# Seven products for one more K tile pair of the second MLP matrix

## The chip, the cores and the metric

The kernel runs on one core of a Trainium2 chip. The metric is the device time of one execution in microseconds (us): the median of several runs. Beside the runs there is one profiled execution, whose trace names each instruction by engine, source line and the tiles it writes and reads (`ps_d<-hi,h` writes ps_d from hi and h). Engines: TensorE (PE; its weight loads are PEld), VectorE (DVE), ScalarE (ACT), GpSimd (POOL) and SyncE (SP), whose queue issues the loads.

## The reference

A decoder trunk of two layers over 256 positions, model width 2048, hidden width 8192, all in float32. Layer 0 mixes by a gated short convolution, layer 1 by latent attention; each is followed by a squared-ReLU MLP. The change touches the two MLPs.

```python
def sq_relu_mlp(x, w1, w2):
    return jnp.square(jax.nn.relu(x @ w1)) @ w2

for layer in range(DEPTH):                       # DEPTH = 2
    mix = short_conv_mixer(...) if layer < N_A else mla_mixer(...)
    h = layer_norm(ALPHA * h + mix, ...)
    h = layer_norm(ALPHA * h + sq_relu_mlp(h, mlp_w1[layer], mlp_w2[layer]), ...)
```

## The kernel before

**Precision.** TensorE multiplies operands of type float32r, which hold fewer bits than float32. So each weight and each activation is kept as a high and a low part, `hi` and `lo` (`split`, L121 on ScalarE and L122 on VectorE), and a product is three matmuls: high times high, high times low, low times high. In `dot` (L283, L284, L285) a 128x128 piece of the activations `h` is the stationary operand and 512 columns of weights stream by. In the products of w1 (`products`, L199 and L203) the weights are stationary and 512 columns (high and low of 256 positions) or 256 columns stream.

**An MLP.** `mlp` goes through the hidden width in eight quarters of 1024 (`NQ` = 8, called quarters here for short, numbered 0 to 7). In each one, eight products of w1 give eight hidden tiles of 128 (`QC` = 8), which alternate between the PSUM banks 0 and 1 and are evacuated by `whole` (L339, L340) and `hidden` into `h`; then w2 brings them down to four blocks of 512 output columns (`NB` = 4), for two halves of 128 positions. The results of all quarters are summed in `acc`.

**Seven products.** In quarters 1 to 6 (`FAST`) the blocks 0 and 1 are done by a form of Strassen's method. A pair j of K tiles, two position halves and two blocks make a product of 2x2 by 2x2 blocks; `fast_products` does it by seven block products (`FACTORS`, named "1" to "7") in place of eight, so by 21 matmuls in place of 24. Four pairs make a quarter. Each named product has a PSUM bank of its own, over all four pairs. The left-hand combinations S1 to S4 are made once a quarter and pair by `form` (L630 to L633, then a split into `forms`); the right-hand ones are made from each pair of raw weight loads in `prepare`: a difference of 1024 columns (L154), two of 512 (L157, L160), three splits of 1024 columns and one of 512 (`t4`).

At the end of this half, `keep` (L588) adds each product to its place: "2", "3" and "4" belong to one output block each and go to `acc`; "1", "5", "7" and "6" (`OWN`) are wanted by several blocks and go to `sums` (in quarter 1 ScalarE copies them). `fold` spreads `sums` over `acc` in the last quarter, one operation per w1 product (L607).

**The direct half.** Blocks 2 and 3 are done by `down`, a block after the other: two PSUM banks (one for each half of positions), eight K tiles, six matmuls each, then `put` (L578) adds both to `acc`. Block 2 uses the banks 1 and 2, block 3 the banks 3 and 4. In the second MLP, in quarters 1 to 4, `turn_residual` transposes the residual between these two blocks on TensorE into the banks 5 and 6 (L945), and VectorE adds them (L946).

**Order.** All weights come as units of 128x1024 through one stream (`mlp_stream` sets its order): SyncE's queue loads a unit into one of five buffers `raw` (L132), ScalarE and VectorE split it into one of eight pairs `hi`, `lo`. `take` hands a unit to TensorE and prepares units up to `LOOK` = 5 ahead, a seven-product pair of units counting three. Each engine works through its own program in order and waits on semaphores; the order in each is set by the scheduler of the framework.

**Memory.** Arrays of the pool `act` lie in the order in which they are first named: c, pad0, b, a1, pad1, a2, pad2. Tag c holds `h`, b the MLP's input `xhl`, a1 `acc` (and earlier half of the input of the opening), a2 `forms`.

## Time and profile before

| | |
|---|---|
| runs | 2025.81 us median of 3 (2025.68 to 2026.14) |
| profiled execution | 2028.49 us, span 2026.4 us |
| granted clock of TensorE | 0.999 of full speed |
| HBM read | 381.25 MB, 189 GB/s over the span |

The span runs from the first to the last instruction; the execution's time holds some us around it. Rows of groups show line, engine, operation, what is written from what, shapes, count, then busy us and the mean of one in ns, then idle time ahead. Rows of the view of time show start and length in us. Rows by stretch show, for each engine, busy us and in brackets the number of instructions, then the granted clock, the DMA share and GB/s. A busy time holds the overlap of neighbours, so the pace of a stream is read from starts.

### The profile page before, as it was taken

The numbers are of one execution on the slowest core, as the hardware profiler recorded it, in microseconds if no ns is written. First come the engines' busy times: TensorE is split into PE (matmuls) and PEld (weight loads), VectorE is DVE, ScalarE is ACT, GpSimd is POOL, SyncE is SP. The second block draws the span as 40 slices with busy tenths as digits, with TensorE's granted clock in tenths as the row PEclk, the third lists the DMA queues.
The fourth block names the chain that finished last, engine by engine and source line by source line (L and its number), as shares of the span: only waits on it lengthen the run. The fifth ranks groups of instructions, "written<-read, shape, count | busy, mean of one in ns | idle before, by whom it ended". The sixth has DMA issues, their size and how long they took to land.

```text
span 2026.4 us, 30052 instructions
## 1 busy us (share of the span) xinstructions
PE 2018.3 (100%) x11240; PEld 1763.1 (87%) x11240; DVE 1605.8 (79%) x2467; ACT 1176.2 (58%) x1797; POOL 2.3 (0%) x21
## 2 busy tenths in 40 slices
PE   9999999999999999999999999999999999999998
PEld 8888888988888888888889998898888888888886
DVE  7667667787787978979678978776879798797966
ACT  6444445576565665656556655566656566565651
POOL 0000000000000000000000000000000000000000
PEclk9999999999999999999999999999999999999999
DMA  8666666564746657475654543656475664746663
GB/s 298 204 188 189 190 187 186 177 196 146 249 148 226 204 170 239 143 240 194 220 179 146 179 134 126 197 177 196 137 249 167 198 227 142 248 160 210 220 201 120
DMA packets 106849, 385.30 MB, mean 190 GB/s; under 512 B 11856, under 2 KB 12752, under 8 KB 106448
## 3 DMA queue, kind: packets, MB, share of 16 engines
q1 hardware_dynamic: 106560, 383.27, 59.3%
q8 instruction: 88, 1.44, 0.3%
q14 instruction: 57, 0.47, 0.1%
q10 hardware_dynamic: 144, 0.13, 0.0%
HBM read 381.25 MB, written 2.10 MB: 189 GB/s over the span
## 4 chain that ended last, share of the span: by engine, by line
PE 99%; DMA 0%; DVE 0%; SPq 0%; issue 0%; ACT 0%; DVEq 0%
PE ps_u L199 20%; PE ps_l L199 13%; PE ps_u L203 11%; PE ps_d L285 7%; PE ps_d L283 7%; PE ps_d L284 7%; PE ps_l L203 7%; PE ps_f L284 4%; PE ps_f L285 4%; PE ps_f L283 4%; PE ps_w L233 2%; PE ps_w L231 2%; PE ps_w L232 2%; PE ps_g L231 1%; PE ps_g L233 1%; PE ps_g L232 1%
## 5 line engine op out<-in xcount | busy, mean ns | idle before, releaser
L122 DVE TENSOR_TENSOR lo<-raw,hi 128x1024 fp32r<-128x1024 f32 x710 | 859.8, 1222 | 314.1 <-ACT hi L121 243.0
L121 ACT CAST hi<-raw 128x1024 fp32r<-128x1024 f32 x710 | 742.4, 1051 | 460.0 <-PE ps_u L199 108.0
L199 PE MATMUL ps_u<-xhl,hi 128*128 128x512 f32 x1792 | 621.0, 391 | 0.0
L203 PE MATMUL ps_u<-xhl,lo 128*128 128x256 f32 x1792 | 499.5, 280 | 0.0
L199 PEld LDWEIGHTS ps_u<-xhl,hi 128*128 128x128 f32 x1792 | 334.2, 187 | 72.4
L203 PEld LDWEIGHTS ps_u<-xhl,lo 128*128 128x128 f32 x1792 | 338.6, 189 | 1.8
L283 PE MATMUL ps_d<-hi,h 128*128 128x512 f32 x640 | 249.8, 390 | 0.0
L285 PE MATMUL ps_d<-hi,h 128*128 128x512 f32 x640 | 249.1, 389 | 0.0
L284 PE MATMUL ps_d<-lo,h 128*128 128x512 f32 x640 | 249.0, 389 | 0.0
L199 PE MATMUL ps_l<-xhl_a,hi 128*128 128x512 f32 x704 | 243.5, 392 | 0.0
L203 PE MATMUL ps_l<-xhl_a,lo 128*128 128x256 f32 x704 | 194.8, 279 | 0.0
L199 PEld LDWEIGHTS ps_l<-xhl_a,hi 128*128 128x128 f32 x704 | 131.7, 187 | 29.5
L283 PEld LDWEIGHTS ps_d<-hi,h 128*128 128x128 f32 x640 | 120.2, 188 | 25.0 <-DVE fh L340 0.3
L285 PEld LDWEIGHTS ps_d<-hi,h 128*128 128x128 f32 x640 | 120.1, 188 | 24.9
L284 PEld LDWEIGHTS ps_d<-lo,h 128*128 128x128 f32 x640 | 120.2, 188 | 24.7
L203 PEld LDWEIGHTS ps_l<-xhl_a,lo 128*128 128x128 f32 x704 | 132.2, 188 | 0.2
L199 PE MATMUL ps_l<-z,hi 128*128 128x512 f32 x240 | 83.9, 398 | 0.0
L641 ACT ACTIVATE fp<-fp 128x256 f32<-128x256 f32 x96 | 40.0, 416 | 72.6 <-DVE fp L340 71.9
L121 ACT CAST hi_t<-raw_t 128x1024 fp32r<-128x1024 f32 x48 | 50.4, 1050 | 42.9 <-DVE raw_t L154 33.4
L233 PE MATMUL ps_w<-xd,hi 128*128 128x258 f32 x256 | 73.0, 285 | 0.0
L231 PE MATMUL ps_w<-xd,hi 128*128 128x258 f32 x256 | 72.6, 284 | 0.0
L232 PE MATMUL ps_w<-xd,lo 128*128 128x258 f32 x256 | 72.4, 283 | 0.0
(257 smaller groups left out, 3134.5 us busy)
## 6 DMA issues: line engine op xcount, KB each, us to landing
raw<-in_w_dram SPq DMA_DIRECT2D x416, 512.0 KB, 4.3
raw<-in_w2f_dram SPq DMA_DIRECT2D x96, 512.0 KB, 3.6
raw<-in_w_in_dram SPq DMA_DIRECT2D x88, 512.0 KB, 3.6
raw<-in_w_out_dram SPq DMA_DIRECT2D x32, 512.0 KB, 3.9
raw<-in_w_o_dram SPq DMA_DIRECT2D x32, 512.0 KB, 4.3
raw<-in_w_kv_dram SPq DMA_DIRECT2D x10, 512.0 KB, 4.2
raw<-in_w_q_dram SPq DMA_DIRECT2D x8, 512.0 KB, 4.5
raw<-in_w_uk_dram SPq DMA_DIRECT2D x8, 512.0 KB, 4.4
```

Source lines behind the costliest of these rows:

```text
L121: nc.scalar.copy(hi, src)
L122: nc.vector.tensor_tensor(lo, src, hi.bitcast(F32), ALU.subtract)
L199: nc.tensor.matmul(ps, w[blk // 8][0][:, blk % 8, :], x, start=first, stop=False)
L203: nc.tensor.matmul(ps[:, :T], w[blk // 8][1][:, blk % 8, :], x[:, :T], start=False, stop=last)
L231: nc.tensor.matmul(ps[:, :W], hi, x[k][:, :W], start=k == 0, stop=False)
L232: nc.tensor.matmul(ps[:, :W], lo, x[k][:, :W], start=False, stop=False)
L233: nc.tensor.matmul(ps[:, :W], hi, x[k][:, W:], start=False, stop=k == NC - 1)
L283: nc.tensor.matmul(ps, x[0], w[0], start=first, stop=False)
L284: nc.tensor.matmul(ps, x[0], w[1], start=False, stop=False)
L285: nc.tensor.matmul(ps, x[1], w[0], start=False, stop=last)
L641: nc.scalar.activation(f, f, AF.Relu)
```

## The change

In quarters 1 to 6 the blocks 2 and 3 are done together, in one pass over the four K tile pairs (`MIXED` = "ppsp"): pairs 0, 1 and 3 directly ("p"), pair 2 by seven products ("s"). The four direct results have banks 1 to 4, and the products "2", "3", "4" of pair 2 go on in the banks of the results they belong to; "1", "5", "7" and "6" get the banks 0, 5, 6, 7 (`OWN_BANKS`). In a direct pair, block 3 comes first, both position halves, then block 2. `sums` holds two sets, and `fold` spreads both, in eight operations of 2x512 columns. The stream carries pair 2 as a seven-product pair of units (`w2f` now holds all blocks), the direct pairs as block 3, then block 2. In one dot of each quarter (`EVEN`: the last K tile's "22") the middle matmul is done in two of 256 columns. `turn_residual` comes after pair 0, into the banks 6 and 7. The arrays of `act` are named in the order c, a2, a1, b without pads, and a scratch area of 4096 bytes is cut to 512.

```diff
+MIXED = "ppsp"
+EVEN = (QC - 1, "22")
...
-    for tag, columns in (("c", 4096), ("pad0", 64), ("b", 8256), ("a1", 4128), ("pad1", 96), ("a2", 4128), ("pad2", 96)):
+    for tag, columns in (("c", 4096), ("a2", 4128), ("a1", 4128), ("b", 8256)):
...
+            out += [(w2f[l, q, 0, j, 0], w2f[l, q, 0, j, 1]) for j in range(QC // 2)]
+            for j, kind in enumerate(MIXED):
+                out += [(w2f[l, q, 1, j, 0], w2f[l, q, 1, j, 1])] if kind == "s" else \
+                    halves(w2[l, q, 3, j]) + halves(w2[l, q, 2, j])
...
-    def dot(ps, w, x, first, last):
+    def dot(ps, w, x, first, last, two=False):
 
         nc.tensor.matmul(ps, x[0], w[0], start=first, stop=False)
-        nc.tensor.matmul(ps, x[0], w[1], start=False, stop=False)
+        for at in (slice(0, T), slice(T, 2 * T)) if two else (slice(None),):
+            nc.tensor.matmul(ps[:, at], x[0], w[1][:, at], start=False, stop=False)
         nc.tensor.matmul(ps, x[1], w[0], start=False, stop=last)
...
     OWN, KEPT = ("1", "5", "7", "6"), (2, 3, 4, 5, 6, 7, 0)
+    OWN_BANKS = (0, 5, 6, 7)
...
-        sums = fast.tile([P, 4, BW], F32, name=f"sums{idx}")
+        sums = fast.tile([P, 4, 2, BW], F32, name=f"sums{idx}")
...
+            ps = {p: psum("ps_d", bank) for p, bank in zip(("22", "3", "2", "4"), (1, *KEPT))}
+            for j, kind in enumerate(MIXED):
+                if kind == "s":
+                    first, last = j == MIXED.index("s"), j == MIXED.rindex("s")
+                    if first:
+                        ps.update({p: psum(f"ps_f{p}", bank) for p, bank in zip(OWN, OWN_BANKS)})
+                    fast_products(ps, h, forms, j, OWN if first else (), OWN if last else ())
+                    if last:
+                        for p in OWN:
+                            keep(p, 1, ps[p])
+                    continue
+                for nb, two in ((3, ((1, "22"), (0, "3"))), (2, ((0, "2"), (1, "4")))):
+                    w, = take(1)
+                    for t, p in two:
+                        for kk in range(2):
+                            k = 2 * j + kk
+                            dot(ps[p], wide_rows(w, kk), held(h[k], t), k == 0, k == QC - 1, (k, p) == EVEN)
+                    if j == n - 1:
+                        for _, p in two:
+                            keep(p, 1, ps[p])
+                if extra and q <= NB and j == 0:
+                    for t in range(2):
+                        extra(block, q - 1, t, KEPT[4 + t])
...
-                first_pair(h, forms, KEPT)
-                for n, banks in ((2, (1, 2)), (3, (3, 4))):
-                    down(h, put, n, banks)
-                    if extra and n == 2 and q <= NB:
-                        for t in range(2):
-                            extra(block, q - 1, t, 5 + t)
+                down_pairs(h, forms)
...
-    nc = _bacc.Bacc("TRN2", target_bir_lowering=False, num_devices=1, dynamic_dma_scratch_size=4096)
+    nc = _bacc.Bacc("TRN2", target_bir_lowering=False, num_devices=1, dynamic_dma_scratch_size=512)
```

More of the change, by code (lines that the diff above doesn't have):

```diff
@@ L83, in mlp_stream @@
             out += halves(w1[l, q * QC:(q + 1) * QC])
-            plain = halves(w2[l, q, 2:] if q in FAST else w2[l, q])
-            fast = [(w2f[l, q, j, 0], w2f[l, q, j, 1]) for j in range(QC // 2)] if q in FAST else []
-            at = 0 if q or q not in FAST else len(plain) // 2
-            out += plain[:at] + fast + plain[at:]
+            if q not in FAST:
+                out += halves(w2[l, q])
+                continue
[3 more added lines that the diff above has]
+                    halves(w2[l, q, 3, j]) + halves(w2[l, q, 2, j])
         return out
@@ L333, in fast_products @@
         for p, l, r in FACTORS:
-            dot(ps[p], b[r], a[l], j == 0, j == n - 1)
+            dot(ps[p], b[r], a[l], p in fresh, p in ready)
     def whole(ps, out):
@@ L588, in keep, with down_pairs @@
                 nc.vector.tensor_tensor(at, at, ps, ALU.add)
-        def first_pair(h, forms, banks):
+        def down_pairs(h, forms):
             n = QC // 2
-            ps = {p: psum(f"ps_f{p}", bank) for (p, _, _), bank in zip(FACTORS, banks)}
+            ps = {p: psum(f"ps_f{p}", bank) for (p, _, _), bank in zip(FACTORS, KEPT)}
             for j in range(n):
-                fast_products(ps, h, forms, j, n)
+                fast_products(ps, h, forms, j, ps if j == 0 else (), ps if j == n - 1 else ())
@@ L599, in fold @@
         def fold():
             s1, s5, s7, s6 = (sums[:, i] for i in range(4))
[L602 to L606 removed]
+            c = acc.rearrange("p t (g b c) -> p t b g c", g=2, b=2)
```

23 lines of the change are left out of this document (12 added, 11 removed).

## The prediction

> **What bounds the kernel now.** I read the page first: the busy times, then the chain that ended last by engine.
>
> ```profile
> span 2026.4 us, 30052 instructions
> PE 2018.3 (100%) x11240; PEld 1763.1 (87%) x11240; DVE 1605.8 (79%) x2467; ACT 1176.2 (58%) x1797; POOL 2.3 (0%) x21
> PE 99%; DMA 0%; DVE 0%; SPq 0%; issue 0%; ACT 0%; DVEq 0%
> ```
>
> TensorE is busy for the whole span and is the chain. Next I asked for the waits of TensorE alone:
>
> ```profile
> PE ps_g L199 <- ACT hi L121: 1.9, 1, 1.9
> PE offset L998 <- DVE udiag L996: 1.2, 1, 1.2
> PE warm L355 <- DVE col L357: 1.1, 1, 1.1
> ```
>
> Three waits, 4.2 us in all, none in the quarters that the change touches. So the time is the number of matmuls times their pace, for as long as VectorE and ScalarE deliver in time. The busy times by stage say how near that is. The rows are, for two quarters of the first MLP in turn, the eight products of w1 and then the two halves of w2 (seven products on blocks 0 and 1, direct on blocks 2 and 3):
>
> ```profile
> core 0: us, PE busy (x) PEld busy (x) DVE busy (x) ACT busy (x) POOL busy (x), PEclk, DMA share, GB/s
> 587.70:606.80 19.10, 19.10 (x87) 15.79 (x86) 17.69 (x24) 11.19 (x15) 0.00 (x0) 1.00 0.53 159
> 606.80:628.50 21.70, 21.70 (x97) 18.00 (x96) 19.11 (x21) 12.63 (x12) 0.00 (x0) 1.00 0.82 290
> 628.50:672.90 44.40, 44.40 (x257) 39.09 (x257) 35.27 (x52) 27.57 (x45) 0.00 (x0) 1.00 0.55 171
> 672.90:692.00 19.10, 19.10 (x86) 15.81 (x85) 17.55 (x25) 12.26 (x16) 0.00 (x0) 1.00 0.54 162
> 692.00:713.80 21.80, 21.80 (x98) 18.05 (x97) 18.92 (x21) 11.59 (x11) 0.00 (x0) 1.00 0.84 314
> ```
>
> VectorE has some 2.8 us free in the direct half and 9.1 us in the 44.4 us of products. The clock is 1.00 throughout.
>
> **What is removed.** The view of time gives TensorE's pace: its rows at the start and the end of a half follow each other without a gap.
>
> ```profile
> 682.72 0.39 PE L284 MATMUL ps_f<-lo,forms 128*128 128x512 f32 x1
> 691.79 0.39 PE L285 MATMUL ps_f<-t,h 128*128 128x512 f32 x1
> 692.01 0.39 PE L283 MATMUL ps_d<-hi,h 128*128 128x512 f32 x1
> ```
>
> From 682.72 to 692.01 are 41 steps: 9.29/41 = 0.2266 us each (the 0.39 is one matmul's own length; they overlap). The third K tile pair of blocks 2 and 3 took 8 dots of 3 matmuls and now takes 7, so 3 go. That happens in six quarters of two layers: 36 x 0.2266 = 8.16 us. In one dot of each quarter a 512 column matmul becomes two of 256. Two such in a row stand in the trace where the w1 products turn their order:
>
> ```profile
> 543.88 0.40 PE L203 MATMUL ps_u<-xhl,lo 128*128 128x256 f32 x2
> 544.12 0.64 PE L199 MATMUL ps_u<-xhl,hi 128*128 128x512 f32 x2
> 544.59 0.28 PE L203 MATMUL ps_u<-xhl,lo 128*128 128x256 f32 x1
> ```
>
> The two take 0.24 us, 0.013 over one of 512, and the two of 512 behind them 0.47, 0.017 over. Cost 0.02 to 0.04 us; I take 0.035, 0.4 us for twelve. The sum for TensorE alone is 7.75 us.
>
> The Trainium skill ("TensorE: Matmul & The Clock Gate", Back-to-back issue gap) gives about 131 ns a matmul at 512 columns for a sustained stream of weight loads and matmuls. By it the saving would be 36 x 0.131 = 4.7 us; this trace's 0.2266 differs and decides.
>
> **What is added, and what hides it.** The third pair's weights now go through the seven-product preparation. Its VectorE operations, from the groups of one half by shape:
>
> ```profile
> L122 DVE TENSOR_TENSOR lo_t<-raw_t,hi_t 128x1024 fp32r<-128x1024 f32 x2 | 2.4, 1222 | 0.0
> L160 DVE TENSOR_TENSOR raw<-raw 128x512 f32<-128x512 f32 x2 | 1.4, 688 | 0.0
> L157 DVE TENSOR_TENSOR raw<-raw,raw_t 128x512 f32<-128x512 f32 x2 | 1.4, 686 | 0.0
> L122 DVE TENSOR_TENSOR t<-raw,t 128x512 fp32r<-128x512 f32 x2 | 1.4, 683 | 0.0
> L154 DVE TENSOR_TENSOR raw_t<-raw,raw 128x1024 f32<-128x1024 f32 x1 | 1.2, 1220 | 0.0
> ```
>
> Added per quarter: L154 1.22, one more split 1.22, three operations of 512 columns at 0.69: 4.5 us. Eight sums instead of four leave PSUM in the direct half, 4 x 0.68 = 2.7 us more (0.68: rows of L588 below). ScalarE gets one more cast of 1024 columns and one of 512. The loads stay two of 512 KB in the same place of SP's queue, from another array. In the direct half VectorE then needs 18.9 + 7.2 = 26.1 us, while TensorE takes 21.1. So 5.0 us are carried into the products, which have 9.1 free: hidden, if no single result comes too late. That is to be followed along VectorE's order, which I read from the changed program. Up to the sum of product 1 it is the order of before, so the trace shows it, at 692.01 as start of the half:
>
> ```profile
> 691.93 1.23 DVE L122 TENSOR_TENSOR lo<-raw,hi 128x1024 fp32r<-128x1024 f32 x1 [1.33 <-ACT hi L121]
> 693.07 0.68 DVE L588 TENSOR_TENSOR sums<-sums,ps_f 128x512 f32<-128x512 f32 x1
> 693.66 1.22 DVE L122 TENSOR_TENSOR lo<-raw,hi 128x1024 fp32r<-128x1024 f32 x1
> 694.80 1.28 DVE L588 TENSOR_TENSOR sums<-sums,ps_f 128x512 f32<-128x512 f32 x2
> 696.00 0.68 DVE L588 TENSOR_TENSOR acc<-acc,ps_f 128x512 f32<-128x512 f32 x1
> 696.59 0.68 DVE L588 TENSOR_TENSOR sums<-sums,ps_f 128x512 f32<-128x512 f32 x1
> 697.19 0.68 DVE L588 TENSOR_TENSOR acc<-acc,ps_f 128x512 f32<-128x512 f32 x1
> ```
>
> A new wait stands here. Banks 3 and 4 held products 1 and 5 and were wanted again only after 48 matmuls; now the direct sums "2" and "4" open them after 12 and 18 matmuls: 12 x 0.2266 = 2.72 us and 4.08 us. Product 1's sum ends at 693.75, 1.74 us into the half: 1.0 us to spare. Product 5 follows at once and ends by 2.4. The sum stands behind a split that waits for ScalarE's cast, which waits for a DMA or for TensorE; all TensorE work would queue behind that. The worst quarter of the trace is the one at 606.78:
>
> ```profile
> 606.78 0.39 PE L283 MATMUL ps_d<-hi,h 128*128 128x512 f32 x1
> 608.21 1.23 DVE L122 TENSOR_TENSOR lo<-raw,hi 128x1024 fp32r<-128x1024 f32 x1 [2.52 <-ACT hi L121]
> 609.35 0.68 DVE L588 TENSOR_TENSOR sums<-sums,ps_f 128x512 f32<-128x512 f32 x1
> ```
>
> There it ends 3.25 us in, 0.5 late. The wait's cost is between 0 and 0.5 us a quarter; one quarter in twelve looks like that one, so I take 0.3 us in all and keep 6 us as its upper bound.
>
> Next is the third pair itself. Step to step VectorE needs 1.14 us for 1024 columns (693.66 to 694.80) and 0.60 for 512 (696.00 to 696.59). After product 1 the six other sums end the queue at 1.65 + 6 x 0.6 = 5.3 us; the chain of the third pair (first split, difference, two of 512, two splits, last of 512) reads 6.4, 7.6, 8.2, 8.8, 9.9, 11.1, 11.7. TensorE begins the pair at 48 x 0.2266 = 10.9 us and wants those splits at 11.1, 12.5, 13.8 and 15.2: 2.6 us or more to spare, 1.1 in the worst quarter. Then follow ten splits of the next products and eight sums up to the first evacuation of a w1 product: 11.7 + 2 x 1.14 + 10 x 1.14 + 8 x 0.6 = 30.2. Bank 0 is wanted again two products later, at 21.1 + 11.1 = 32.2 (a product is 44.4/8 = 5.55): 2 us to spare, 0.5 in the worst. By the eighth product the 5 us are worked off. So I put these at nothing; without that cover the cost is the 5.0 us carried over, per quarter.
>
> In the second MLP the turned residual goes to banks 6 and 7 after 24 matmuls rather than 48. Products 2 and 6 have left those by 3.5 and 4.1 us by the same spacing, against 5.4. The final fold gets eight operations of 1024 columns for four of 512 and two of 1024: 9.8 - 5.2 = 4.6 us in 44 us of products with 9 free, twice.
>
> **The other arrays.** Without pads, one array alone (a1: the first half of the opening's input, the accumulator, half of an attention input) changes its place relative to the others within 512 bytes. The trace shows the same loop at two paces with inputs in the same place (below), so place is not what it shows to matter; bounds 0 and, for the opening's 48 column blocks with eight K tiles each from a1, 384 pairs x 0.0076 = 2.9 us. I take 0.
>
> **Sum.** 8.16 - 0.4 - 0.3 = 7.5 us. The profiled execution took 2028.49 us, 2.1 around its span of 2026.4, and would take 2021.0; it stands 2.7 above the median of 2025.81, so the median becomes 2018.3.
>
> **The rivals.** First, the bank wait bites in most quarters: 12 x 0.5 = 6 us eaten, 2024.0. For it: VectorE's order there is fixed and its split waits for others. Against: a typical quarter has 1.0 us to spare.
>
> Second, the products of w1 fall into the slower pace. Pairs of one 512 and one 256 matmul:
>
> ```profile
> 299.79 0.40 PE L199 MATMUL ps_l<-z,hi 128*128 128x512 f32 x1
> 302.27 0.40 PE L199 MATMUL ps_l<-z,hi 128*128 128x512 f32 x1
> 559.62 0.39 PE L199 MATMUL ps_u<-xhl,hi 128*128 128x512 f32 x1
> 561.70 0.39 PE L199 MATMUL ps_u<-xhl,hi 128*128 128x512 f32 x1
> ```
>
> Seven pairs in 2.48 us against six in 2.08: 0.3543 and 0.3467. If the new end of the half tips the twelve stages behind it, 12 x 128 x 0.0076 = 11.7 us are lost: 2025.8 - 7.5 + 11.7 = 2030.0. Against: the split stands 18 matmuls of 512 ahead of the stage, and each quarter's matmuls change by an even number.
>
> Third, slower: VectorE's lead is gone before the third pair, so the 5.0 us are not carried but waited for. It decides once the chain above starts 2.6 us later than worked out. Price 12 x 5.0 = 60 us less 7.5: 2078. For it: VectorE would be busy for 93% of a quarter (35.27 + 17.55 + 18.92 + 7.2 of 85.3 less 0.7). Against: the margins above.
>
> Fourth, a bank wait in each quarter is followed by a stretch at a lower granted clock, as one row of the opening has it:
>
> ```profile
> 10.00:15.00 5.00, 4.80 (x18) 4.22 (x19) 4.80 (x13) 4.79 (x15) 0.00 (x0) 0.68 1.05 431
> ```
>
> Five us at 0.68 lose 1.6; twelve lose 19: 2025.8 - 7.5 + 19 = 2037. Against: a wait of half a us would have to do it, and all stages quoted above stand at 1.00. The Trainium skill ("TensorE: Matmul & The Clock Gate", A second HAM failure mode: psum-queue depth-cycling) tells of such a kernel, whose short idles between groups in changing banks let the clock swing; nothing here shows it yet.
>
> That the change does not do what it says (a1's place costs the whole bound) gives 2021.2, within the first range.
>
> **How the numbers follow.** Forecast 2017.0 to 2021.5: 0.76. Bank waits, 2021.5 to 2026: 0.10. Slower pace: 0.06. VectorE late: 0.05. Clock: 0.03. The range 2017.0 to 2023.0 holds the first and half of the second. A change of 0.2% (4.05 us), about what this kernel's runs can tell, needs less than 2021.8 or more than 2029.9. Faster 0.77 (the forecast and a little of the second), same 0.12 (the rest of the bank waits, half of the slower pace), slower 0.11 (the other half, VectorE, clock).
>
> **What would show it.** Right: 11216 matmuls, the direct half 0.65 us shorter, no TensorE wait over 0.5 us at the direct sums, VectorE near 1695 us (1605.8 + 12 x 7.2 + 2 x 4.6, less what ScalarE copies). Wrong: TensorE waiting at the direct sums of bank 3, at the third pair's splits, or at a w1 product's bank; or 0.354 us a pair in the w1 stages.

## The result and the profile after

The changed kernel takes 2029.78 us, the median of 20 runs, against 2026.14 us for the kernel before in the same session: a ratio of 1.0019 (95% interval 1.0012 to 1.0025), 3.6 us slower where 7.5 us less were forecast. Its runs also lie further apart: 2026.82 to 2033.91 us, while those of before lie between 2025.66 and 2026.60, apart from a single one of 5211.27.

The page of the profiled execution after, the busy times and the chain by engine:

```profile
PE 2014.6 (99%) x11216; PEld 1756.3 (87%) x11216; DVE 1682.4 (83%) x2571; ACT 1191.9 (59%) x1829; POOL 2.3 (0%) x21
PE 84%; DVE 9%; DMA 3%; issue 2%; ACT 1%; SPq 0%; DVEq 0%; ACTq 0%
```

The 24 matmuls are gone from the count (36 less, 12 more by the two-part matmul), and VectorE's busy time is near the 1695 us forecast. But the chain has left TensorE: 9% of it is now VectorE and 3% DMA, where before had 0% of each. TensorE's waits, in us, times, and the longest:

```profile
PE ps_u L204 <- DVE fp L347: 2.3, 3, 1.1
PE ps_d L288 <- DVE sums L596: 2.1, 4, 0.9
...
PEld ps_d L288 <- ACT hi L126: 4.6, 6, 1.3
PEld ps_u L204 <- DVE fp L347: 3.8, 5, 1.5
```

Both kinds of place are named: a direct sum that opens a bank (ps_d), and a w1 product that opens one (ps_u); the weight load of such a matmul (PEld) shows the same stall, put down to the cast that came last. The stretches that answer to those of before, and one of the second MLP as the last:

```profile
583.60:602.68 19.08, 19.08 (x87) 15.77 (x85) 18.06 (x24) 11.40 (x17) 0.00 (x0) 1.00 0.54 163
602.68:624.12 21.44, 21.39 (x95) 17.44 (x94) 19.55 (x23) 11.41 (x12) 0.00 (x0) 1.00 0.65 223
624.12:668.52 44.40, 44.40 (x258) 39.15 (x257) 39.31 (x57) 28.55 (x47) 0.00 (x0) 1.00 0.60 199
668.52:687.60 19.08, 19.08 (x87) 15.78 (x85) 18.89 (x26) 12.31 (x17) 0.00 (x0) 1.00 0.52 153
687.60:709.86 22.26, 21.37 (x95) 17.44 (x94) 19.89 (x25) 11.62 (x12) 0.00 (x0) 1.00 0.67 230
1754.10:1799.91 45.81, 44.66 (x258) 39.15 (x256) 41.23 (x60) 29.68 (x47) 0.00 (x0) 1.00 0.60 197
```

The direct half should take 21.11 us (93 steps of 0.2266 and the split); here it takes 21.44 and 22.26. The w1 stage of the last row takes 45.81 instead of 44.39. Added up over the trace from the first matmul of each stage to the first of the next:

| | before | after |
|---|---|---|
| up to the first w1 stage with two banks | 458.07 | 454.62 |
| twelve direct halves, turned residual included | 264.7 | 261.4 (256.9 without a wait) |
| fourteen w1 stages, over 44.39 each | 0.0 | 6.8 |

So the halves save 7.8 us and give 4.5 back in waits, and the w1 stages give back 6.8: 11.3 us lost against 7.8 saved. The 3.45 us at the start are no gain of the mechanism: 2.7 of them lie in the opening's first groups, which took 26.3 us in the profile of before, 23.6 in that of after, and between 23.3 and 26.4 in the profiles of the experiments, whatever their arrays, and before's profiled execution was some 2.4 us over its own median. That of after (2027.96 us) was 1.8 under its median, so in a common run the waits are probably larger than in this trace.

### The profile page after: what moved, and what is told of

It is laid out like the page before. It is cut to its first block, busy times and chain, and to the rows that moved or that the text cites. A ratio compares the mean times of both kernels' runs of the same rounds, so it can differ in the third digit from the quotient of the medians.

```text
span 2026.2 us, 30145 instructions
## 1 busy us (share of the span) xinstructions
PE 2014.6 (99%) x11216; PEld 1756.3 (87%) x11216; DVE 1682.4 (83%) x2571; ACT 1191.9 (59%) x1829; POOL 2.3 (0%) x21
## 4 chain that ended last, share of the span: by engine, by line
PE 84%; DVE 9%; DMA 3%; issue 2%; ACT 1%; SPq 0%; DVEq 0%; ACTq 0%
PE ps_u L204 16%; PE ps_l L204 13%; PE ps_u L208 8%; PE ps_l L208 7%; PE ps_d L288 6%; PE ps_d L291 5%; PE ps_d L290 5%; DVE lo L127 3%; DMA raw<-in_w_dram 3%; PE ps_f L291 3%; PE ps_f L290 3%; PE ps_f L288 3%; PE ps_w L238 2%; PE ps_w L236 2%; PE ps_w L237 2%
## 5 line engine op out<-in xcount | busy, mean ns | idle before, releaser
L288 PE MATMUL ps_d<-hi,h 128*128 128x512 f32 x556 | 218.2, 392 | 2.3 <-DVE sums L596 2.1
L291 PE MATMUL ps_d<-hi,h 128*128 128x512 f32 x556 | 216.8, 390 | 0.0
L290 PE MATMUL ps_d<-lo,h 128*128 128x512 f32 (+1 forms) x568 | 216.7, 385 | 0.0
L288 PEld LDWEIGHTS ps_d<-hi,h 128*128 128x128 f32 x556 | 104.5, 188 | 26.4 <-ACT hi L126 4.6
L290 PEld LDWEIGHTS ps_d<-lo,h 128*128 128x128 f32 x568 | 106.7, 188 | 21.7
L291 PEld LDWEIGHTS ps_d<-hi,h 128*128 128x128 f32 x556 | 104.4, 188 | 21.5
L126 ACT CAST hi_t<-raw_t 128x1024 fp32r<-128x1024 f32 x60 | 62.8, 1047 | 97.6 <-DVE raw_t L159 96.7
L159 DVE TENSOR_TENSOR raw_t<-raw,raw 128x1024 f32<-128x1024 f32 x60 | 73.2, 1220 | 7.6 <-DMA raw<-in_w2f_dram 7.4
L127 DVE TENSOR_TENSOR lo_t<-raw_t,hi_t 128x1024 fp32r<-128x1024 f32 x60 | 73.2, 1220 | 1.2
L238 PE MATMUL ps_w<-xd,hi 128*128 128x258 f32 x256 | 72.8, 285 | 0.0
```

What stands on the lines that cost most here:

```text
L126: nc.scalar.copy(hi, src)
L127: nc.vector.tensor_tensor(lo, src, hi.bitcast(F32), ALU.subtract)
L159: nc.vector.tensor_tensor(t.rearrange(two, a=2), b12.unsqueeze(1).to_broadcast([P, 2, BW]), r1.rearrange(two, a=2), ALU.subtract)
L238: nc.tensor.matmul(ps[:, :W], hi, x[k][:, W:], start=False, stop=k == NC - 1)
L288: nc.tensor.matmul(ps, x[0], w[0], start=first, stop=False)
L290: nc.tensor.matmul(ps[:, at], x[0], w[1][:, at], start=False, stop=False)
```

## The experiments

Times are medians; every call had runs of the kernel before on the same chip, which came out between 2026.14 and 2026.50 us. "Lost" is what a profile shows over the lengths without a wait: in the twelve direct halves, and in the w1 stages. It holds for the profiled execution, which lies within 2 us of the median but for three runs: that of "both" took 2031.24 us, 5.5 over its median, that of "layout4" 3.9 over, that of "pool2" 4.4 over. "onet4" lost another 1.3 us in the twelve seven-product halves, "pool" and "pool2" 15.5 each.

| run | us | range | ratio to before (95%) | lost: halves, w1 |
|---|---|---|---|---|
| after | 2029.78 | 2026.8 to 2033.9 | 1.0019 (1.0012 to 1.0025) | 4.5, 6.8 |
| banks | 2029.69 | 2026.9 to 2031.7 | 1.0016 (1.0007 to 1.0024) | 9.3, 3.7 |
| order | 2029.70 | 2027.8 to 2033.7 | 1.0016 (1.0007 to 1.0025) | 0.0, 13.4 |
| both | 2025.78 | 2020.5 to 2033.0 | 0.9998 (0.9990 to 1.0007) | 1.9, 12.0 |
| layout | 2026.47 | 2025.5 to 2028.8 | 1.0001 (0.9993 to 1.0010) | 0.2, 0.0 |
| dose12 | 2028.46 | 2027.7 to 2029.8 | 1.0012 (1.0003 to 1.0021) | 3.7, 0.0 |
| prep | 2033.16 | 2031.7 to 2033.8 | 1.0033 (1.0020 to 1.0046) | 4.8, 2.7 |
| nosums | 2024.03 | 2022.2 to 2028.5 | 0.9989 (0.9980 to 0.9997) | 1.4, 3.9 |
| raw6 | 2018.77 | 2018.3 to 2020.6 | 0.9963 (0.9951 to 0.9976) | 1.4, 0.0 |
| raw6order | 2018.13 | 2017.7 to 2018.9 | 0.9960 (0.9945 to 0.9975) | 1.4, 0.0 |
| onet4 | 2032.95 | 2031.9 to 2035.2 | 1.0034 (1.0022 to 1.0045) | 12.1, 1.9 |
| early | 2038.51 | 2036.9 to 2043.3 | 1.0064 (1.0051 to 1.0077) | 23.6, 0.4 |
| place | 2025.07 | 2024.7 to 2027.2 | 0.9995 (0.9986 to 1.0004) | 0.0, 0.0 |
| place6 | 2028.29 | 2027.0 to 2032.3 | 1.0012 (1.0003 to 1.0022) | 2.2, 0.0 |
| layout4 | 2031.38 | 2030.4 to 2035.2 | 1.0029 (1.0019 to 1.0040) | 5.1, 0.0 |
| even | 2030.92 | 2027.4 to 2034.2 | 1.0023 (1.0014 to 1.0032) | 6.4, 9.5 |
| stall | 2032.48 | 2031.3 to 2033.6 | 1.0032 (1.0022 to 1.0043) | 0.0, 5.1 |
| pool | 2103.22 | 2102.4 to 2103.9 | 1.0380 (1.0366 to 1.0394) | 47.8, 22.5 |
| pool2 | 2102.37 | 2101.6 to 2106.7 | 1.0375 (1.0361 to 1.0390) | 49.0, 24.7 |

### Give the two places more room: banks, order, both

If the fault were the two late hand-overs of banks, other banks and another order would cure it. "banks":

```diff
-                for m, ps in enumerate(products(QC, xhl, TURNED, (0, 1))):
+                for m, ps in enumerate(products(QC, xhl, TURNED, (0, 5, 6, 7, 0, 5, 0, 1))):
```

> After, but the eight products of each w1 stage take banks 0, 5, 6, 7, 0, 5, 0, 1 in turn instead of 0 and 1; nothing else. Theory (VectorE enters each seven-product half some 1.7 us later than before and so evacuates late; a TensorE wait at a w1 product's bank also tips that stage into the slower pace): no wait at a w1 product's bank, every w1 stage at 44.4 us, which takes away the 6.8 us that six such stages of the profile had over it; the waits at bank 3 of the direct half stay (4 to 5 us). 2029.8 - 6.8 = 2023.0, at most 2024.5. Rival (VectorE is simply too late; the wait moves on to the next thing it delivers): the w1 stages stay long, 2028 to 2030.

"order" (the stream is reordered to match, and the turned residual follows block 3):

```diff
                 for nb, two in ((3, ((1, "22"), (0, "3"))), (2, ((0, "2"), (1, "4")))):
-                    w, = take(1)
...
+                    for i in (0, 1) if j == 0 else (j,):
+                        w, = take(1)
...
```

> After, but the first two K tile pairs of blocks 2 and 3 are taken block by block (block 3 of both pairs, then block 2 of both), so that banks 3 and 4 open 24 and 36 matmuls into the half (5.44 and 8.2 us) instead of 12 and 18. Theory: no wait at bank 3 any more, the first part of the direct half is 10.9 us in each quarter (4.5 us less in all); but TensorE then comes earlier to the w1 products, whose banks 0 and 1 are still handed on late, so part or all of it comes back there with the slower pace behind it: 2026 to 2030. Rival (the two waits are independent of each other): 2029.8 - 4.5 = 2025.3 or less, w1 stages as long as in the profile of after.

> Both of these edits together. Theory (the lost time is these two bank waits and the pace behind them): all direct halves 21.1 us, all w1 stages 44.4, 2029.8 - 4.5 - 6.8 = 2018.5, at most 2020. Rival (VectorE has too much work for its place, and the wait moves to the third pair's splits or to the splits of w1): waits there of 0.3 us or more in half of the quarters, 2022 to 2027.

Neither alone gained anything. TensorE's waits in "banks", then in "order":

```profile
PE ps_d L288 <- DVE sums L596: 7.1, 7, 1.6
PE ps_u L204 <- DVE fp L347: 2.2, 4, 1.3
```

```profile
PE ps_u L206 <- DVE fp L349: 4.3, 3, 2.2
```

With more banks in w1 the waits grew at the direct sums, from 4.5 to 9.3 us of the halves. With the direct sums out of the way (their halves all at 21.11 in the first MLP) they came back twice as large in w1, 13.4 us, some 1.6 of it by a stretch at a lower clock (last section). The profiles lose 13.0 us in "banks" and 13.4 in "order", that of after 11.3: the wait moves to wherever VectorE's result is wanted next. Both edits together did gain: 4.0 us less than after in the median, with intervals that don't overlap, and runs from 2020.5 to 2033.0; the 13.9 us of the profile belong to one of the slowest of them. So the two margins are part of the loss, but with both widened most of it stayed: my theory, which had 2018.5, fell in its size, and the rival holds, that VectorE is late as such.

### Where VectorE is late: layout, dose12, prep, nosums

"layout" keeps the one pass, the eight banks and their early opening, and leaves out the third pair's seven products:

```diff
-MIXED = "ppsp"
+MIXED = "pppp"
-EVEN = (QC - 1, "22")
+EVEN = (QC, "22")
```

> After with the third pair of blocks 2 and 3 computed directly like the others (8 dots instead of 7, no preparation, no second set of four sums, no two-part matmul); the one pass over both blocks with banks 1, 2, 3, 4, the order of the arrays and the products' banks stay as in after. Theory (VectorE's 4.5 + 2.7 us a quarter make it late): bank 3 is ready as in the traced halves of before, 1.0 us ahead; no wait over 0.3 us there in most quarters, w1 stages at 44.4: the time of before or up to 2 us less, 2024 to 2026.5. Rival (opening banks 3 and 4 so early is a wait by itself, whatever VectorE has to do): waits of 0.3 us or more at bank 3 in most quarters, 2028 or more.

No wait came (0.2 us in all halves), and the time is that of before: opening banks 3 and 4 early costs nothing while VectorE has before's work. "dose12" then puts the change's time on VectorE back, and nothing else of it:

```diff
+                if j == 1:
+                    for i in range(12):
+                        nc.vector.tensor_tensor(sums[:, i % 4, 1, :], block(0, 0), block(0, 0), ALU.add)
```

> The kernel of the run 'layout' (all of the third pair direct, no waits, 2026.5) with twelve operations of 512 columns put into VectorE's order at the place of the second pair, 12 x 0.6 = 7.2 us a quarter, into a buffer that nobody reads. Theory (VectorE's added time alone makes the loss): the evacuations lag by 5 us and more and TensorE waits at bank 3 and at w1 banks from the second or third quarter of each MLP on; 4 to 11 us slower than 'layout', 2030 to 2037. Rival (the third pair's loads and casts, or its earlier wants of banks 0, 5, 6, 7, make the loss): 2028 or less.

It lost 2.0 us by the medians (3.5 by the two profiles), less than the theory's least of 4 and close to the rival's most: VectorE's busy time (1684.6 us) is that of after, and most of the loss is missing. "prep" has the same time on VectorE by the change's own preparation: the third pair is loaded and prepared as for seven products, with four such operations beside it, and TensorE's stages stay as in "layout":

```diff
-                out += [(w2f[l, q, 1, j, 0], w2f[l, q, 1, j, 1])] if kind == "s" else \
+                out += [(w2f[l, q, 1, j, 0], w2f[l, q, 1, j, 1])] if j == 2 else \
...
+                    b, = take(1)
+                    for i in range(4):
+                        nc.vector.tensor_tensor(sums[:, i % 4, 1, :], block(0, 0), block(0, 0), ALU.add)
```

> The run 'layout' (5 raw buffers) with the third pair of blocks 2 and 3 loaded and prepared as for seven products, three raw buffers held as in after, plus four operations of 512 columns for the four sums: VectorE's and ScalarE's work and the buffers are those of after, while TensorE still does 8 dots with no further banks. The third pair's dots take prepared differences in place of plain weights, so that part of the result is not the reference's. Theory R (the held buffers, beside VectorE's time, make the lag): clearly more lost than the 2.0 us of 'dose12', which had the same time on VectorE and no buffer held: 2030.5 or more. Rival V (VectorE's time alone; after loses more only because its stages are 0.65 us shorter and its banks wanted earlier): as 'dose12', 2027.5 to 2029.5.

6.7 us over "layout", with VectorE busy for 1677.1 us, less than in "dose12". So VectorE's busy time alone doesn't set the loss; the preparation costs by what else it brings: raw buffers held, casts that wait for VectorE, and another order on both engines. One row of ScalarE's waits differs between the two, first in "dose12" and then in "prep":

```profile
ACT hi_t L126 <- DVE raw_t L159: 33.3, 12, 2.8
```

```profile
ACT hi_t L126 <- DVE raw_t L159: 96.0, 24, 6.0
```

The cast of a pair's difference stands in ScalarE's order until VectorE has written the difference; with a third pair it stands there twice as often and up to 6.0 us long, and the casts of plain weights queue behind it. After has the same row with 96.7, 24 and 6.0, before 33.4, 12 and 2.8. Three raw buffers are held meanwhile. The standing by itself isn't the loss: "raw6" below keeps twelve such waits of up to 6.6 us, 66.5 in all, and loses only 1.4 us.

VectorE's time still counts where the rest is given. "nosums" leaves out the sums of the third pair after the first such quarter:

```diff
-                    if last:
+                    if last and q == 1:
```

> After, but the four product sums of the third pair are added only in the first such quarter of each MLP and left out in the others: VectorE has 4 x 0.6 = 2.4 us less in ten quarters. This leaves a part of the result out. Theory V: the lag per quarter shrinks by up to 2.4 us and most of the waits go: 2020 to 2024. Theory R: the loads are as late as before, 2027 to 2030.

5.7 us less than after, for 2.4 us in each of ten quarters.

### The raw buffers: early, raw6, onet4, place6, layout4

```diff
-        t4 = r1[:, :BW]
+        t4 = t[:, :BW]
```

> After, but a pair's last difference (t4) is written into the first half of the buffer t instead of the first half of the first load's buffer r1, which so comes free some 3 us sooner for the next load; no work is added or removed. Theory R (VectorE's idle time is the five raw buffers: the third pair holds three of them to the end of its preparation, the loads behind start late, and VectorE stands in order behind a cast that waits for them): VectorE's waits for casts shrink, evacuations lag less, 2022 to 2026. Rival V (VectorE's added work, and stages 0.65 us shorter, alone set its lag): 2029 to 2030.5, as after.

It went the other way, to 2038.51 us. One buffer comes free sooner, but the last difference now stands behind the cast and the split of t, and the other two come free later; the run neither speaks for theory R nor against it.

```diff
-RAW, WA = 5, 8
+RAW, WA = 6, 8
...
-        f = state["fast"].tile([P, 2, BW], F32R, tag="t4", name=f"t4_{i}", bufs=2)
+        f = state["fast"].tile([P, 2, BW], F32R, tag="t4", name=f"t4_{i}", bufs=1)
```

> After with six raw buffers instead of five, paid for with one t4 buffer instead of two. Theory R: one more load under way, the casts wait less for loads, lag at the first evacuation back to 3 to 4 us: 2019 to 2024. Rival V: no change beyond what the missing t4 buffer costs, 2029 or more.

2018.77 us: with as many instructions on each engine, 11 us less than after and 7.7 less than before, within 0.5 us of the time that I had forecast for the change. The page, the only wait in the MLPs that the view of TensorE's waits names, and one quarter of the second MLP (w1, seven products, direct half):

```profile
PE 2008.8 (100%) x11216; PEld 1755.1 (87%) x11216; DVE 1676.3 (83%) x2571; ACT 1198.3 (59%) x1829; POOL 2.3 (0%) x21
PE 96%; DVE 2%; DMA 1%; issue 0%; ACT 0%; SPq 0%; DVEq 0%
```

```profile
PE ps_d L288 <- DVE acc L596: 0.4, 1, 0.4
```

```profile
1748.50:1792.89 44.39, 44.39 (x258) 39.12 (x256) 36.91 (x55) 27.18 (x43) 0.00 (x0) 1.00 0.53 178
1792.90:1811.98 19.08, 19.08 (x87) 15.77 (x86) 18.42 (x26) 13.60 (x19) 0.00 (x0) 1.00 0.59 188
1811.98:1833.50 21.52, 21.41 (x96) 17.43 (x95) 21.45 (x27) 10.63 (x11) 0.00 (x0) 1.00 0.68 242
```

VectorE has as much to do as in after and is no longer late: in the direct half it is busy for 21.45 of 21.52 us, in after for 19.55 of 21.44 and 19.89 of 22.26. What changed is how long ScalarE's casts stand waiting for a load, in after and then in "raw6":

```profile
ACT hi L126 <- DMA raw<-in_w_dram: 126.4, 131, 3.6
```

```profile
ACT hi L126 <- DMA raw<-in_w_dram: 62.9, 92, 2.5
```

Half of that waiting is gone. Before had 87.6 us of it. (The row by itself is no measure of the loss: in "dose12" it has 165.3 us, where the twelve operations in a row hold up the buffers.) The edit has two parts, so each was tried by itself or elsewhere. "onet4" has the single t4 buffer without the sixth raw buffer:

> After with one t4 buffer instead of two, and five raw buffers as in after: the half of the run 'raw6' that pays for the sixth. Theory R (the sixth raw buffer alone makes the 11 us of 'raw6'): the time of after or more, 2029 to 2034. Rival (one t4 buffer changes VectorE's order for the better): 2019 to 2024.

"place6" gives both to "place", the kernel before with the new order of the arrays (below), which has no waits to lose:

> The run 'place' (before with the arrays in the new order) with six raw buffers and one t4 buffer, as in 'raw6'. TensorE has no wait there to lose. Theory: 2025.1 within 0.7, so that with six buffers the change itself is worth 2025 less 2018.8 = 6.3 us, about what 36 matmuls and the waits left over make. Rival (a sixth buffer speeds up the kernel as such, by another way than the waits of the change): 2022 or less.

The single t4 buffer costs 3.2 us in after and the pair of edits costs 3.2 in the kernel "place". So the sixth raw buffer is worth 14.2 us (2032.95 less 2018.77) where the third pair is prepared, while the same two edits make the kernel without it no quicker. One reserve: VectorE's order follows from the buffers and is another one in each of these versions. In "raw6" the sums of products 3 and 1 follow each other without a split between:

```profile
1811.72 1.23 DVE L127 TENSOR_TENSOR lo<-raw,hi 128x1024 fp32r<-128x1024 f32 x1 [0.53 <-ACT hi L126]
1812.87 0.68 DVE L596 TENSOR_TENSOR acc<-acc,ps_f 128x512 f32<-128x512 f32 x1
1813.46 1.87 DVE L596 TENSOR_TENSOR sums<-sums,ps_f 128x512 f32<-128x512 f32 x3
```

How much of the gain comes with that order wasn't separated from the earlier loads.

"layout4" (`RAW, WA = 4, 8` in "layout") takes a buffer away where VectorE has nothing more to do:

> The run 'layout' (the third pair direct, no added work on VectorE, no waits) with four raw buffers instead of five. Theory R (what a quarter can carry is set by the loads through the raw buffers, not by VectorE's time): the waits of after come back without any added work, at the direct sums and at w1 banks, VectorE's busy time unchanged: 2032 or more. Rival V (VectorE's time sets it): 2026 to 2028, as 'layout'.

4.9 us are lost by the medians at an unchanged busy time (1608.2 us), but not where the theory said. The profile, the slowest of the eight runs, shows none in the first MLP, 5.1 us in the second around the turned residual, and about as much in the attention, which also loads through these buffers. That fewer buffers cost time is shown; that they alone make after's picture isn't.

"raw6order" joins "raw6" and "order":

> The run 'raw6' with blocks 2 and 3 taken block by block over the first two pairs, as in the run 'order'. With the loads in time, the rest of the waits at the direct sums (1.4 us in the profile of 'raw6') has 2.7 us more room: 2017.4 to 2018.5. Rival (TensorE, no longer held there, meets the late evacuation in w1 instead): 2018.8 or more.

2018.13 us (17.7 to 18.9) is the least of all, though the 1.4 us in the halves that it was to take away are still there: at best 0.6 us better than "raw6", and their ranges overlap. I had them at the wrong place: in "raw6" TensorE waits six matmuls into the half, where "3" opens bank 2 behind the evacuation of product 3, and "order" opens that bank no later.

### The pace, the arrays, GpSimd: stall, even, place, pool

In after, five of the fourteen w1 stages run at 0.354 us a pair from their third product on, 0.65 to 0.7 us each. "stall" makes a wait at the same place in the kernel before:

```diff
-                for m, ps in enumerate(products(QC, xhl, TURNED, (0, 1))):
+                for m, ps in enumerate(products(QC, xhl, TURNED, (0, 0, 1, 0, 1, 0, 1, 0))):
```

> Before, but the second product of each w1 stage goes into the bank of the first (0, 0, 1, 0, 1, 0, 1, 0), so that TensorE has to wait there once in each of fourteen stages, some 2.5 us. Theory (a TensorE wait inside a w1 stage tips the pairs behind it into the slower pace): the six products behind the wait at 0.354 us a pair instead of 0.347 in most stages, 0.7 us a stage beside the wait. Rival (the slower pace in after is chance or comes from something else): 0.347 behind the waits too.

The view of time of "stall" around such a place, in the w1 stage that starts at 541.77:

```profile
546.99 0.39 PE L199 MATMUL ps_u<-xhl,hi 128*128 128x512 f32 x1
...
549.76 0.39 PE L199 MATMUL ps_u<-xhl,hi 128*128 128x512 f32 x1
549.99 0.28 PE L203 MATMUL ps_u<-xhl,lo 128*128 128x256 f32 x1
550.12 0.19 PEld L199 LDWEIGHTS ps_u<-xhl,hi 128*128 128x128 f32 x1 [0.16 <-DVE fp L340]
550.12 0.50 PE L199 MATMUL ps_u<-xhl,hi 128*128 128x512 f32 x1
550.46 0.28 PE L203 MATMUL ps_u<-xhl,lo 128*128 128x256 f32 x1
550.57 0.40 PE L199 MATMUL ps_u<-xhl,hi 128*128 128x512 f32 x1
...
553.40 0.40 PE L199 MATMUL ps_u<-xhl,hi 128*128 128x512 f32 x1
```

Eight pairs ahead take (549.76 - 546.99)/8 = 0.346 us, eight behind (553.40 - 550.57)/8 = 0.354. The first product ends at 547.34, but its bank is opened again only at 550.12: by the count of matmuls, eight pairs of another product have been put between. So the wait that I expected at 2.5 us was next to none: the matmul at 550.12 starts 0.13 us after the last one, and the step behind it is 0.34 long instead of 0.23. Thirteen stages tipped at this place and one at the next such hand-over, 48 matmuls on, each where a bank just let go was opened; the thirteen fell back to 0.347 two or three products later, by what wasn't found. That TensorE opens a bank so soon after its product, and not the late release, does it isn't excluded here; in after the product had ended 5.55 us before.

"even" leaves out the two-part matmul (`EVEN = (QC, "22")`):

> After without the two-part matmul: the half has an odd number of matmuls. Theory (TensorE's pace in a w1 stage goes by how the stage is entered): w1 stages without a wait take 44.4 us in one quarter and 45.2 in the next; since VectorE's lag eats what TensorE gains, the time is that of after within 3 us. Rival (the split does nothing for the pace): all stages without a wait at 44.4, 0.4 us less than after.

The w1 stages at 455.2 and 539.7, and those at 1412.3 and 1497.8, all stand at 44.39 with an odd number of matmuls between them: no parity shows. The halves without a wait take 21.08 instead of 21.11, so the split costs 0.03 us, as I had put it, and buys nothing that shows here.

"place" has only the arrays' order and the small scratch:

> Before with only the new order of the arrays (no pads) and the smaller scratch. Theory (the 384 pairs with z run at the quicker pace for it, as in the profile of after, and nothing else moves): 1 to 3 us less than before. Rival (the place of the arrays means nothing, the pace there is chance): the time of before, within 0.5 us.

The stage of the products with z, in "place" and in before:

```profile
280.09:363.30 83.21, 83.21 (x482) 73.36 (x481) 63.21 (x103) 44.68 (x61) 0.00 (x0) 1.00 0.64 187
```

```profile
281.57:366.35 84.78, 84.78 (x482) 73.58 (x481) 63.92 (x103) 44.61 (x61) 0.00 (x0) 1.00 0.62 185
```

1.57 us less in that stage, 0.65 more in the products of the opening ahead of it (245.17 for 244.52): 0.9 us less in all, and so it is in each of the eighteen profiles with the new order against the two with the old, before and "stall". The time is 1.25 us less, though the interval of the ratio reaches 1.0004.

"pool" moves the four small operations of `form` to GpSimd, and "pool2" issues their split still later:

```diff
-                nc.vector.tensor_tensor(s1, a21, a22, ALU.add)
+                nc.gpsimd.tensor_tensor(s1, a21, a22, ALU.add)
...
```

> After, but the four 128x128 operations that build the sums of a pair's factors (sf) run on GpSimd instead of VectorE, and their two-part split is issued one product later; VectorE has 16 x 0.2 to 0.28 = 3.2 to 4.5 us less to do in each quarter. Theory (VectorE has no usable time for the 7.2 us that the change adds; its lag, not the banks, is the cause, so the waits only moved in the two runs with other banks and another order): with half of the dose gone the first evacuation of a w1 product lags its end by 3.5 us or less instead of 5 to 6.6, no wait over 0.3 us at bank 3 or at a w1 bank: 2018 to 2020. Rival (the lag is that of loads through the five raw buffers and of casts behind them, so less work on VectorE buys nothing, or GpSimd is so slow that VectorE waits for it): 2026 or more.

> The run with the factor sums on GpSimd again, with their two-part split issued a further product later (that of the last pair inside the seven-product half), since there GpSimd's four operations took 3.6 us in a row and VectorE and ScalarE waited for them in each pair. VectorE has 3.2 to 4.5 us less per quarter. Theory V: half of the dose gone, 2020 to 2025. Theory R: VectorE's work does not matter, 2028 to 2030. Third: GpSimd's chain still stops the queues: over 2035.

Both took 2102 to 2107 us. GpSimd's groups in "pool", and VectorE's split of the hidden tile between 700 and 1000 us, in after and in "pool":

```profile
L660 POOL TENSOR_TENSOR sf<-fp 128x128 f32<-128x128 f32 x48 | 52.3, 1089 | 242.1 <-ACT fp L677 242.1
```

```profile
L127 DVE TENSOR_TENSOR h<-fp,h 128x512 fp32r<-128x512 f32 x12 | 8.2, 685 | 0.0
```

```profile
L127 DVE TENSOR_TENSOR h<-fp,h 128x512 fp32r<-128x512 f32 x12 | 11.4, 950 | 0.0
```

An operation that VectorE does in 0.29 us took GpSimd 1.09, and VectorE's split beside it grew from 0.69 to 0.95 us. The Trainium skill ("SBUF — State Buffer", Who interferes with whom) says that a VectorE instruction with two inputs in SBUF and a GpSimd instruction that reads SBUF hold each other up; the row agrees. ScalarE's cast of the sums waited for GpSimd 2.0 us in each of the 48 pairs (97.4 us), with all casts of weights behind it. The runs say nothing on VectorE's time.

## Why the prediction was wrong

**TensorE's saving: right.** 11216 matmuls, and a direct half without a wait takes 21.11 us for 21.76, 12 x 0.65 = 7.8 us. With six raw buffers the kernel reaches 2018.77; the forecast was 2018.3. That these lie so close is in part luck: the order of the arrays gives 0.9 us that I had put at nothing, and 1.4 us of waits are left. The granted clock stayed at 1.00 in the stages of after; the fourth rival didn't come there. By the rule of the Trainium skill ("TensorE: Matmul & The Clock Gate", Back-to-back issue gap), about 131 ns a matmul, the estimate for the 36 was 4.7 us; the halves without a wait show 7.8.

**VectorE's added work: right in size, wrong in when it can be done.** 1682.4 us against 1695. The step that failed is this: "In the direct half VectorE then needs 18.9 + 7.2 = 26.1 us, while TensorE takes 21.1. So 5.0 us are carried into the products, which have 9.1 free: hidden, if no single result comes too late", and with it the chain worked out behind it, where each step of VectorE follows the last without a gap. It lets VectorE fill the 2.8 us that it stood idle in the direct half. In after it didn't: it is busy for 19.2 us of a direct half on average and idle for 2.6, in before for 19.2 and 2.8. VectorE's waits in the half that starts at 692.01 in before, and in the one that starts at 687.60 in after:

```profile
DVE lo L122 <- ACT hi L121: 4.2, 4, 1.5
```

```profile
DVE lo L127 <- ACT hi L126: 2.3, 4, 1.5
```

VectorE stands in its order behind a split whose cast hasn't come, and in both the casts wait mostly for loads (5.8 and 6.1 us in these two halves). Over the twelve halves these waits of VectorE's come to 34.8 us in before, 34.7 in after and 4.4 in "raw6", where VectorE is idle for 0.4 us a half. So nearly the whole 7.2 us of added work, and not 5.0, was pushed behind the half. The 9.1 us in the products were for the most part what I took them for. VectorE's waits in that stage of before (628.5 to 672.9), and in that of after (624.1 to 668.5):

```profile
DVE lo L122 <- ACT hi L121: 8.7, 7, 1.5
```

```profile
DVE lo L127 <- ACT hi L126: 4.0, 4, 1.4
```

In before the casts there waited for TensorE (7.7 us), so VectorE was ahead of it, and after did use about half of that time: it is busy for 39.31 us there instead of 35.27, 4.9 more on average over quarters 2 to 6. But the results came too late for the banks, and in after the casts wait for loads there too (3.7 us, where before has none). The loads are the term that I had put at nothing, with no more said than that they "stay two of 512 KB in the same place of SP's queue": the third pair holds three of five raw buffers while it is prepared, and leaves two to the loads behind it. Beside that it has casts that wait for VectorE themselves; since "raw6" keeps the longest of these and loses only 1.4 us, the buffers weigh more. Nor were the 5 us "worked off" by the eighth product. That VectorE entered the next seven products late, the evacuation of the last w1 product shows, before and then after, 2.3 us into the half that starts at 672.93 and 4.1 into the one that starts at 668.52:

```profile
675.24 0.42 DVE L340 TENSOR_TENSOR fp<-ps_u,t 128x256 f32<-128x256 f32 x1
```

```profile
672.59 0.42 DVE L347 TENSOR_TENSOR fp<-ps_u,t 128x256 f32<-128x256 f32 x1
```

The experiments divide the loss roughly. After's time without any wait would be some 2017.3 us ("place" less the 7.75 of TensorE's sum), so 12.5 are lost. By the medians VectorE's time alone makes 2.0 of them ("dose12"), the preparation around it 4.7 more ("prep"); the other 5.8, by that subtraction alone (4.4 if it starts from "layout", whose median is 1.4 over that of "place"), I put down to stages 0.65 us shorter and banks wanted sooner. No run shows that part by itself.

**Product 1's sum: the mechanism seen, the place right, the size wrong.** I gave it 1.0 us to spare in a typical quarter and 0.3 us of loss in all. In after, in the quarter whose half starts at 687.60:

```profile
688.32 1.05 ACT L126 CAST hi<-raw 128x1024 fp32r<-128x1024 f32 x1 [2.29 <-DMA raw<-in_w_dram]
...
689.40 1.23 DVE L127 TENSOR_TENSOR lo<-raw,hi 128x1024 fp32r<-128x1024 f32 x1 [1.52 <-ACT hi L126]
...
690.54 1.88 DVE L596 TENSOR_TENSOR sums<-sums,ps_f 128x512 f32<-128x512 f32 x3
...
691.37 0.47 PE L288 MATMUL ps_d<-hi,h 128*128 128x512 f32 x1 [0.89 <-DVE sums L596]
```

Read from top to bottom: a load comes late, the cast waits 2.29 us for it, the split 1.52 us for the cast, the three sums stand behind the split, and TensorE waits for the first of them, which ends 3.6 us into the half and was wanted at 2.72. VectorE isn't short of time here; it stands idle for 1.52 us just ahead. In the traced quarter of before the same split started 0.08 us ahead of the half, here 1.80 behind its start. That is the third rival's condition, VectorE's lead gone, but not its price: no half of after shows a wait at the third pair's splits. I had taken the lateness of the worst quarter of before as an outlier of one in twelve; in after eight of twelve halves wait there, 4.5 us in all.

**The first evacuation of a w1 product: the second margin, whose cost I put at nothing.** I had it end 30.2 us after the start of the direct half, with bank 0 wanted at 32.2. In the stage that starts at 1754.10 (the half before it at 1731.80):

```profile
1760.37 5.76 DVE L127 TENSOR_TENSOR lo<-raw,hi 128x1024 fp32r<-128x1024 f32 x5
...
1763.75 1.05 ACT L126 CAST hi<-raw 128x1024 fp32r<-128x1024 f32 x1 [1.47 <-DMA raw<-in_w_dram]
...
1766.05 0.42 DVE L347 TENSOR_TENSOR fp<-ps_u,t 128x256 f32<-128x256 f32 x1
...
1766.52 0.50 PE L204 MATMUL ps_u<-xhl,hi 128*128 128x512 f32 x1 [1.15 <-DVE fp L347]
```

It ends at 1766.47, 34.7 us after the start of the half, 4.5 later than worked out; TensorE, whose half is 1.2 us longer than 21.11 (0.9 of it the turned residual), wanted the bank at 1765.2. VectorE works without a gap from 1756.84 on, at the end through five splits in a row; it had lost its time before, in the half, where it was idle for 3.3 us behind casts.

**The slower pace** was my second rival, given 0.06, with another cause. No end of a half tips a stage; a bank handed over late, or just in time, inside it does, in five stages of six where that happened. It adds 0.65 to 0.7 us to each of the five, about half of what w1 lost. I had held the rivals apart; what makes the first brings the second with it. **The arrays' place** I took as 0, since two paces with inputs in the same place seemed to clear it; the traces give 0.9 us for it, 1.57 gained in the stage with z less 0.65 lost in the opening. **The two-part matmul** costs 0.03 us each, as put. **The turned residual and the fold** showed no wait of their own in after.

The first rival (2024.0) and the second (2030.0) both came true in part, with 4.5 and some 3.4 of the 11.3 us in after's trace; I had given them 0.16 together. The other 3.4 are waits at the banks of w1 products, which I had named as a sign of being wrong but given no price of their own.

## What to carry to other kernels

Idle time of an engine in order is spare only as far as what it stands waiting for comes no later; ask of each idle stretch what ended it, down to the load or the engine behind it, and whether the added work holds up that very thing. Here the idle time that waited for TensorE took work in, and the idle time that waited for loads did not. Where two tight places are fed by the same late engine, widening one moves the wait to the other: the sum of the waits tells that sooner than either. The profile of a kernel whose runs lie far apart shows one of them, so compare its time with the median before using its waits. A change that prepares more data through the same buffers should be tried with one buffer more before it is given up: here that turned 0.2% slower into 0.4% faster.

## What the hardware showed beside that

TensorE's stream of a 512 and a 256 column matmul has two paces, 0.347 and 0.354 us a pair, with the same instructions. A hand-over of a bank that costs some 0.12 us over two steps was enough to change it, in all fourteen stages of "stall", and the slower one stayed for two to six products, 64 to 192 matmuls. The same two paces showed in the stage with z (83.21 and 84.78 us), there with the order of the arrays: all eighteen profiles with the new order have the one, those of before and "stall" the other.

A longer wait can be followed by a lower granted clock. One of 2.2 us at a w1 bank in "order", in the view of time and in the stretch behind it:

```profile
1679.13 0.64 PE L206 MATMUL ps_u<-xhl,hi 128*128 128x512 f32 x1 [2.20 <-DVE fp L349]
...
1679.79 0.63 PE L206 MATMUL ps_u<-xhl,hi 128*128 128x512 f32 x1
```

```profile
1679.00:1683.00 4.00, 3.87 (x13) 3.29 (x14) 2.84 (x5) 2.87 (x5) 0.00 (x0) 0.57 0.99 371
```

For some 3.5 us a pair takes 0.64 us, at a mean clock of 0.57 over the 4 us shown. The waits of up to 1.5 us in after left the stages that hold them at 1.00. The length alone doesn't decide it: in "early", waits of 2.21 us (868.48) and of 2.58 us (1746.97) left the clock at 1.00 over the 4 us behind them, and what decides wasn't found.
